# A GLA + RWKV-7 layer on one core: the state's share of y moved to array quarters at the end of a head pair

## The chip, the core and the metric

The kernel runs on one core of one Trainium2 chip, in one launch. The time is the device time of an execution in microseconds (us). The kernel before took 1492.62 us (median of 3 runs, 1492.28 to 1493.64).

A core has five engines with a queue each. The profile calls them PE (TensorE, matrix products; PEld is its loading of weights), DVE (VectorE), ACT (ScalarE), POOL (GpSimd) and SP (SyncE, which here issues the DMAs). A queue is worked off in order. Matrix products land in PSUM, eight banks of 128 partitions by 512 float32; the other operands lie in SBUF.

## What is computed

One layer of a decoder over 1024 prompt tokens and 8 single-token samples, width 1024, all in float32:

- `p = x @ w_in`, 9360 columns, split into the inputs of two branches and two gates.
- a gated linear attention branch (GLA) with 4 heads;
- an RWKV-7 branch with 16 heads of 64: for every token `S = S (diag(w) - kk^T (kk * a)) + v^T k` and `y = S r`, where `w = exp(-0.606531 * sigmoid(...))` is a decay for each channel. Then y is normalised, scaled, and a bonus is added;
- both branches are multiplied by `silu` of their gates, projected up, merged under sigmoid gates, projected by `w_out`, and normalised with the residual.

Outputs are y for prompt and samples, and the final states of both branches.

## The kernel before

**Tiling.** Tokens run along the free dimension, channels on the 128 partitions. There are two passes: 512 prompt tokens and the 8 samples, then 512 prompt tokens. Large products split each float32 operand into two parts of TensorE's faster 32-bit format (`xh`, `xl` of x; a two-part `wpart` of the weights) and add three products. They are the `proj<-xh,wpart` and `proj<-xl,wpart` groups of the profile.

**The RWKV branch.** Two heads make a pair, head 0 on partitions 0 to 63 and head 1 on 64 to 127. There are 8 pairs a pass, 16 in all. A pair's 512 tokens are cut into 8 chunks of 64 (`NCH`, `C`). Within a chunk the recurrence is solved as a block system, so that only the state goes from chunk to chunk. A pair goes through these functions:

- `front` (L1128 on). Sigmoids give the decay's logarithm; a scan along each chunk sums it (`tb`, started anew at each chunk by the mask `reset`); `Pc`, with 65 columns a chunk, is `exp` of minus the sum from the chunk's start, and `tb` becomes `exp` of plus the sum. `AZ` holds, for each chunk, three slots of 64 columns: the removal key times its decay, r of head 0 and r of head 1 times theirs. The last two are each zero on the other head's partitions; those zeros are written once at the start. `BK` holds the two right-hand factors divided by their decay, `pc` the decay over a whole chunk. Then the masked matrices: for 4 chunks at a time, two banks (one for each head) take 8 matmuls on 64 rows of the array, and VectorE multiplies them by a mask into `GG` (tile `gg`). Corner blocks of `GG` go through memory (`LD`) to POOL, which solves them token by token; the result returns to `XT`.
- `back` completes the inverse, and copies slot 0 of `AZ` over the diagonal blocks of `GG[:, :, 0]` (the off-diagonal ones hold the masked matrix).
- `turn` transposes `BK` and v. `d.u` is a tile of [128, chunk, head, 65]: on a head's partitions, under its own index, lies the state, and on the other partitions lies v.
- `chain` (L1303 on) goes through the chunks in order. For each: `pr = GG[:, x, 0] . u`, copied to `rh`; `pY = u . AZ[:, x, 1:]`, one full-array matmul of 128 rows, 128 columns and 128 streamed columns, which is the state's share of y for both heads (thanks to the zeros); `s0`, the state times `pc`, on ScalarE; `pu = XT . rh`, copied into u; `pS = BK . u`; and the next state, `pS * pc + s0`. `pY` keeps two PSUM banks for the length of a chain. When all chunks are done, 16 matmuls on column halves of the array (`pY<-gg,wide`) add the tokens' share of y in one uninterrupted group, and four copies bring y to SBUF.
- `norm` normalises y and stores it to `o_rwkv`, which is read again much later for the up-projection.

**Order.** Nothing in the program's text fixes the order between streams. `Order.run` is a planner: each stream (`pair`, `chain`, `evacuate`, GLA `head`, weight loads `w`, projections `block` and so on) offers its next operation, `price` estimates its duration, `start` the moment at which operands, buffers and engine are free, and the operation with the earliest start less its priority is written next into its engine's queue. The constants at the top (`HOP`, `PRIO`, `FOR_PE`, `SCARCE`, `URGENT` and others) are what it weighs. Operations of `E` may go to DVE or POOL, those of `C` to ACT or DVE. `together` makes one operation of a list of matmuls, so that nothing comes between them. `SWITCH` is the planner's price for a change of the array's tiling.

**Buffers.** `SBUF` names the tags and counts; `row` ([128, 520], 38 of them) serves nearly everything. `BANKS` shares out the PSUM banks: 2 `proj`, 3 `big`, 1 `pch` for the chain, 2 `pY`. `get(tag, n)` waits until n buffers are free at once; `get_of` takes the free one of several tags.

Of the kernel before, what the change touches and what calls it, by code (L numbers as in the profile page):

```python
# [20 lines left out]
P = 128  # L21
D = 1024
# [25 lines left out]
    "row": ([P, HALF], 38), "wide": ([P, NCH * 2 * CV], 4), "gg": ([P, 4 * HT], 2), "lw": ([P, HT], 2),  # L48
    "l2s": ([P, 2 * P], 1), "pc": ([P, NCH], 3), "X": ([P, 256], 1),
    "Xt": ([P, P], 1), "Ld": ([P, P], 2), "S": ([P, GDV], 2), "Sp": ([P, CV], 2), "s0p": ([P, 2 * CV], 2), "rh": ([P, 2 * CV], 2), "vm": ([P, NCH], 2),  # L50
# [5 lines left out]
BANKS = {"proj": 2, "big": 3, "pch": 1, "pY": 2}  # L56

KEEP = 3
# [7 lines left out]
SPARE_ROWS = 10  # L66
EARLY_GATES = 11


HOP = {"P": 0.2, "D": 0.339, "G": 0.12, "V": 0.064, "A": 0.14}  # L70
# [5 lines left out]
AGE = 0.851  # L76

SPARE = 0.315
LANDED = 0.337
BIAS = 0.174  # L80
ASIDE = 1.32

PRIO = {"evacuate": 0.48, "pair": 0.3, "turn": 0.5, "chain": 0.5, "norm": 0.1, "x": 0.69, "lora": 0.08, "rank":
        -0.15, "head": 0.3, "gate": -0.13, "w": 0.3, "out": -0.17, "state": 0.16, "block": 0.09}
FOR_PE = {"pair": 0.92, "turn": 1.49, "chain": 1.0, "norm": 0.76, "lora": 0.29, "rank": 1.96, "head": 1.0, "gate":
        1.0, "state": 1.85, "out": 0.05}
STAND, SCARCE, PER_ROW = 0.034, 0.227, 0.083

URGENT = 0.981
# [61 lines left out]
def price(eng, name, out, args, ins):  # L151

    n = out.free_size()
    src = [x for x in ins if x.tensor.space != PSUM] if eng == "A" else ins
    if eng == "P":
        m = args[0].free_size()
        rows, cols = tiles(name, args)
        if name == "transpose":
            return 0.1095
        if args[0].dtype == F32R:  # L160
            return max(m / 1200, 0.0045 + n / 2256) if rows == cols == P else (m + n) / 1200
        if rows == cols == P:
# [266 lines left out]
class Kern(Order):  # L429
# [71 lines left out]
    def setup(self):  # L501
# [64 lines left out]
        self.reset = cp.tile([P, HT], U8, name="reset")  # L566
        nc.vector.memset(self.reset, 1)
        nc.vector.memset(self.reset[:, ::C], 0)


        for tag, n, bufs in (("az", 3 * HT, 2), ("XT", 2 * HT, 2), ("Yd", HT, 1), ("Xd", HT, 1)):
# [132 lines left out]
    def blocks(self):  # L704
        xs = None
        for b in self.plan:
# [17 lines left out]
            for tt, (t0, n) in enumerate(tiles):  # L724
                fin = tt == len(tiles) - 1
                ps = yield from (self.get("proj") if b.src is self.a["w_in"] else self.get_of("proj", "pY", "big"))
# [19 lines left out]
    def first_blocks(self, xs):  # L746

        run = []
        for b in self.plan[:2]:
            evac = yield from b.act()  # L750
            for tt, (t0, n) in enumerate(b.c.tiles):
                ps = yield from self.get_of("proj", "pY", "big")
# [375 lines left out]
    def front(self, c, p, st, d):  # L1128
# [4 lines left out]
        AZ, GG = az.rearrange("p (c s t) -> p c s t", c=NCH, s=3), gg.rearrange("p (c k h t) -> p c k h t", c=NCH, k=2, h=2)  # L1133
# [14 lines left out]
        ta, tb, td, te = (x[:, :HT] for x in (ta, tb, td, te))  # L1148
        Pc_ = Pc_[:, :NCH * (C + 1)]
        Pc = Pc_.rearrange("p (c t) -> p c t", t=C + 1)  # L1150
# [3 lines left out]
        yield A.activation(ta, pw, AF.Sigmoid, bias=self.pvec("w0", p))  # L1154
# [19 lines left out]
        for h, hs in enumerate(HS):  # L1174
            yield E.tensor_mul(AZ[hs, :, 1 + h], bc(r)[hs], Pc[hs, :, 1:])
        pc = yield from self.get("pc")
        yield E.tensor_copy(pc, Pc[:, :, C])

        for h, hs in enumerate(HS):
            yield E.tensor_mul(BK[hs, :, h * C:h * C + C], bc(td)[hs], bc(tb)[hs])  # L1180
            yield E.tensor_mul(BK[hs, :, C - h * C:2 * C - h * C], bc(kb)[hs], bc(tb)[hs])
# [67 lines left out]
    def back(self, d):  # L1249
# [24 lines left out]
        for h, hs in enumerate(HS):  # L1274
            yield self.C.copy(GG[hs, :, 0, h], d.AZ[hs, :, 0])
# [27 lines left out]
    def chain(self, c, p, d):  # L1303
# [9 lines left out]
        S, pYs = (yield from self.get("Sp")), []  # L1313

        for x in range(NCH):
            u = u_[:, x]
            uf = u.rearrange("p h v -> p (h v)")[:, 1:1 + P]
            if x % 4 == 0:
                pYs.append((yield from self.bank("pY", [P, 4, 2, C])))
# [21 lines left out]
            self.free(pS, s0p)  # L1341
        uf = u_.rearrange("p c h v -> p c (h v)")
        yield together([self.P.matmul(pYs[x // 4][hs, x % 4, h], uf[:, x, 1 + h * C:1 + h * C + C], GG[:, x, 1, h], start=False,
                                      stop=True, skip_group_check=True) for x in range(NCH) for h, hs in enumerate(HS)])
        for x, pY in enumerate(pYs):
            cs = slice(4 * C * x, 4 * C * x + 4 * C)
            for h, hs in enumerate(HS):
                yield self.C.copy(d.y[hs, cs].rearrange("p (c t) -> p c t", t=C), pY[hs, :, h])
            self.free(pY)
# [199 lines left out]
    def load_out(self):  # L1549
# [4 lines left out]
        ln1 = yield from self.get("Yd")  # L1554
        self.lnv = [[ln[:, 0:512], ln[:, 512:D]], [ln[:, D:], ln1]]
# [27 lines left out]
    def out(self, c, xs):  # L1583
# [3 lines left out]
        for t0, x0 in rows:  # L1587
# [6 lines left out]
            for n, (c0, cn) in enumerate(parts):  # L1594
                ps = yield from self.get_of("proj", "pY", "big")
# [22 lines left out]
    def out_sample(self, xs):  # L1618
# [10 lines left out]
        for j in range(2):  # L1629
            ps = yield from self.get_of("proj", "pY", "big")  # L1630
# [205 lines left out]
```

## Time and profile before

| | |
|---|---|
| median of 3 runs | 1492.62 us |
| profiled execution | 1492.24 us |
| its span, first to last instruction | 1490.5 us |
| busy PE / DVE / ACT / POOL | 1472.6 / 1068.1 / 820.8 / 399.7 us |
| granted TensorE clock, mean | 0.998 of full speed |
| DMA | 319.08 MB, mean 214 GB/s |

A row of groups of instructions reads: line, engine, operation, output<-inputs by tile names, tiling of the array where it is a matmul (rows*columns), shape, count | busy us, mean ns of one | idle time of the engine before them and who ended it. Nearly all instructions carry L225, the planner's helper, so tiles tell them apart. A float32 matmul leaves two records, one for each of its passes. Matmuls are pipelined: a record's own duration contains the depth of the pipeline, and the pace is read from starts. A row of stretches reads: from:to, length, then busy us and count for PE, PEld, DVE, ACT and POOL, granted clock, DMA share and GB/s.

### The profile page before, as it was taken

The page shows a single profiled execution, that of the slowest core. Times are in us where ns is not written, and L with a number is a line of the kernel's source. Part 1 is how long each engine was busy: PE and PEld are TensorE (multiplying, and loading weights), DVE is VectorE, ACT ScalarE, POOL GpSimd, SP SyncE. Part 2 cuts the span into 40 slices and gives each one's busy share as a digit, 9 for nine tenths or more (in the row PEclk, how much of TensorE's full clock was granted, in tenths as well). Part 3 has the DMA queues.
Part 4 walks back from the last instruction along what each step waited for, and adds up shares of the span by engine and source line. Part 5 has one row for each costly group of instructions (what it writes and reads, how often), then busy time and mean ns, then how long its engine had stood idle before and what let it go on. Part 6 is the DMA issues. An engine that isn't in the chain of part 4 may idle for free.

```text
span 1490.5 us, 29705 instructions
## 1 busy us (share of the span) xinstructions
PE 1472.6 (99%) x10308; PEld 1304.6 (88%) x10308; DVE 1068.1 (72%) x2196; ACT 820.8 (55%) x2098; POOL 399.7 (27%) x1154
## 2 busy tenths in 40 slices
PE   9999999999999999999999999999999999999997
PEld 8899999999999998788887888888888898897786
DVE  6688688858796788766557696978586846566665
ACT  5646766766676667544644464464456555643210
POOL 1060605133503442064223505140523050000000
PEclk9999999999999999999999999999999999999999
DMA  8786886787668875764555465746564868787432
GB/s 295 255 285 215 274 280 207 247 263 267 219 195 268 290 248 177 239 203 137 175 182 172 140 184 192 215 131 209 186 219 144 250 185 282 259 293 241 142 113 85
DMA packets 211312, 319.08 MB, mean 214 GB/s; under 512 B 91699, under 2 KB 107196, under 8 KB 211164
## 3 DMA queue, kind: packets, MB, share of 16 engines
q1 hardware_dynamic: 211164, 317.20, 66.3%
q8 instruction: 82, 1.34, 0.4%
q14 instruction: 66, 0.54, 0.1%
HBM read 197.45 MB, written 118.61 MB: 212 GB/s over the span
## 4 chain that ended last, share of the span: by engine, by line
PE 89%; DVE 4%; DMA 3%; SPq 1%; issue 1%; ACT 1%; POOL 0%; POOLq 0%; DVEq 0%; ACTq 0%
PE proj L225 56%; PE big L225 19%; PE pY L225 8%; PE pch L225 6%; DVE row L225 1%; SPq L225 1%; DVE wpart L225 1%; DVE wide L225 1%; DMA row<-w_out 0%; DMA wraw<-w_in 0%; DMA row<-lora 0%; DMA row<-xT 0%; ACT wpart L225 0%; DMA wide<-Sp 0%; DMA row<-mg 0%
## 5 line engine op out<-in xcount | busy, mean ns | idle before, releaser
L225 PE MATMUL proj<-xh,wpart 128*128 128x264 f32 (+2 forms) x3744 | 914.0, 328 | 1.6 <-DVE row L225 1.1
L225 PEld LDWEIGHTS proj<-xh,wpart 128*128 128x128 f32 x3744 | 623.9, 189 | 51.9 <-issue 4.0
L225 PE MATMUL proj<-xl,wpart 128*128 128x264 f32 (+2 forms) x1872 | 616.1, 329 | 0.0
L225 PEld LDWEIGHTS proj<-xl,wpart 128*128 128x128 f32 x1872 | 353.6, 189 | 25.0 <-issue 2.4
L225 POOL TENSOR_TENSOR Xt<-X,wide 128x60 f32<-128x60 f32 (+24 forms) x496 | 168.0, 339 | 483.4 <-DMA wide<-LD 172.8
L225 DVE TENSOR_TENSOR wpart<-wraw,wpart 128x512 fp32r<-128x512 f32 x209 | 147.0, 705 | 67.8 <-ACT wpart L225 63.1
L225 ACT CAST wpart<-wraw 128x512 fp32r<-128x512 f32 x210 | 130.2, 621 | 113.5 <-PE proj L225 68.3
L225 DVE TENSOR_TENSOR row<-row 128x512 f32<-128x512 f32 (+10 forms) x343 | 178.6, 532 | 13.2 <-ACT row L225 6.9
L225 POOL TENSOR_TENSOR X<-X,Xt 128x60 f32<-128x60 f32 (+24 forms) x496 | 173.5, 350 | 38.6
L225 ACT ACTIVATE row<-row 128x512 f32<-128x512 f32 (+4 forms) x229 | 137.9, 611 | 19.8 <-DMA row<-sg 8.4
L225 DVE SCALAR_TENSOR_TENSOR wide<-pch,pc,s0p 64x65 f32<-64x65 f32 x224 | 63.3, 283 | 82.7 <-PE pch L225 80.1
L225 ACT COPY rh<-pch 128x130 f32<-128x130 f32 x125 | 33.5, 268 | 126.1 <-PE pch L225 125.6
L225 DVE SCALAR_TENSOR_TENSOR row<-proj,pv,row 128x255 f32<-128x255 f32 (+1 forms) x97 | 55.5, 572 | 48.5 <-ACT tail L225 33.3
L225 POOL TENSOR_TENSOR row<-row 128x256 f32<-128x256 f32 (+3 forms) x26 | 28.1, 1090 | 227.7 <-DVE row L225 125.6
L225 PE MATMUL big<-row 128*128 128x128 f32 (+4 forms) x464 | 84.8, 316 | 0.5 <-DMA row<-lora 0.5
L225 ACT COPY wide<-pch 64x65 f32<-64x65 f32 x244 | 50.6, 207 | 57.7 <-PE pch L225 53.0
L225 ACT ACTIVATE row<-proj,omu 128x256 f32<-128x256 f32 (+1 forms) x97 | 53.0, 547 | 49.6 <-PE proj L225 47.0
L225 POOL TENSOR_SCALAR XT<-XT,st 128x256 f32<-128x256 f32 x1 | 1.2, 1223 | 267.2 <-ACT st L225 267.2
L225 PE MATMUL big<-xh,wpart 128*128 128x512 f32 (+2 forms) x288 | 68.9, 323 | 0.0
L225 PEld LDWEIGHTS big<-row 128*128 128x128 f32 (+3 forms) x464 | 59.6, 175 | 7.6 <-ACT row L225 1.7
L407 ACT ACT_TABLE_LOAD x50 | 64.2, 1283 | 0.9
L225 PE MATMUL pY<-xh,wpart 128*128 128x256 f32 (+2 forms) x240 | 56.9, 317 | 1.3 <-ACT wpart L225 1.1
(269 smaller groups left out, 2360.7 us busy)
## 6 DMA issues: line engine op xcount, KB each, us to landing
w<-wpart SPq DMA_DIRECT2D x146, 512.0 KB
wpart<-w SPq DMA_DIRECT2D x146, 512.0 KB
wraw<-w_in SPq DMA_DIRECT2D x146, 256.0 KB
wide<-LD SPq DMA_DIRECT2D x64, 128.0 KB
wraw<-w_up_gla SPq DMA_DIRECT2D x32, 256.0 KB
wraw<-w_up_rwkv SPq DMA_DIRECT2D x32, 256.0 KB
sg<-row SPq DMA_DIRECT2D x16, 260.0 KB
row<-sg SPq DMA_DIRECT2D x16, 260.0 KB
```

Source lines behind the costliest of these rows:

```text
L225: ways.append((eng, lambda call=call: call(out, *args, **kw), price(eng, name, out, args, ins)))
L407: self.nc.scalar.preload_act_table_set(self.table)
```

## The change

The decay factors of a pair are now taken relative to a chunk's **end**. The scan runs backwards over 65 columns a chunk (the 65th is set to zero), `Pc` is `exp` of plus the sum, `tb` of minus it, and `pc` is the first column of `tb`. `AZ` has two slots, its zeros are no longer needed, and r is multiplied for both heads in one instruction.

In `chain` the full-array `pY` matmul is gone. `s0` (state times `pc`) is kept for every chunk: it is written over `GG[:, x, 0]`, which the chunk's first matmul has read by then (`gg` gets 65 columns for 64 to hold it). At the end of the chain 16 matmuls of 64 rows, 64 columns and 64 streamed columns, one for each chunk and head, give the state's share of y. They stand in one group with the 16 half-column matmuls of before, into one `big` bank taken only then, and one copy brings y out. `AZ`'s removal keys are multiplied by `pc` when they are put into `GG`, and the next state is a plain sum.

The masked matrices of a pair are made in one group of 16 matmuls over four banks at once, where there were two groups of 8 over two banks each. Beside that: `big` has 5 banks and `pY` none, `row` has 40 buffers, `KEEP` is 0, `SPARE_ROWS` and `EARLY_GATES` are one more, the tag `s0p` is gone, the planner's constants are others, and `price` has a case for 64 by 64. The tiles for the last normalisation's weights follow `az`'s new size (`Yd` and `Xd` in place of the third part of `az`).

```diff
-    "row": ([P, HALF], 38), "wide": ([P, NCH * 2 * CV], 4), "gg": ([P, 4 * HT], 2), "lw": ([P, HT], 2),
+    "row": ([P, HALF], 40), "wide": ([P, NCH * 2 * CV], 4), "gg": ([P, NCH * 4 * CV], 2), "lw": ([P, HT], 2),
...
-BANKS = {"proj": 2, "big": 3, "pch": 1, "pY": 2}
-KEEP = 3
+BANKS = {"proj": 2, "big": 5, "pch": 1}
+KEEP = 0
...
-        return 0.1365 if cols == P else (0.0625 if cols == 64 else 0.142 if n > P else 0.088) if rows == P else 0.5
+        return 0.1365 if cols == P else (0.0625 if cols == 64 else 0.142 if n > P else 0.088) if rows == P else 0.0625 if rows == cols == 64 else 0.5
...
-        yield V.tensor_tensor_scan(tb, self.reset, ta, 0.0, ALU.mult, ALU.add)
-        yield E.memset(Pc[:, :, 0:1], 1.0)
+        yield V.tensor_tensor_scan(tb[:, ::-1], self.reset, ts[:, ::-1], 0.0, ALU.mult, ALU.add)
...
-        yield A.activation(Pc[:, :, 1:], bc(tb), AF.Exp, scale=-LAM)
-        yield A.activation(tb, tb, AF.Exp, scale=LAM)
+        yield A.activation(Pc_, tb, AF.Exp, scale=LAM)
+        yield A.activation(tb, tb, AF.Exp, scale=-LAM)
...
+        yield E.tensor_mul(AZ[:, :, 1], bc(r), Pc[:, :, 1:])
...
-        for h, hs in enumerate(HS):
-            yield E.tensor_mul(AZ[hs, :, 1 + h], bc(r)[hs], Pc[hs, :, 1:])
...
-        for x in range(0, NCH, H):
-            ps = yield from self.get("big", 2)
-            ps = [y.rearrange("p (c k t) -> p c k t", c=H, k=2) for y in ps]
-            yield together([self.P.matmul(ps[h][:, n], BK[hs, x + n], AZ[hs, x + n, 0:2 + h:1 + h], start=True, stop=True)
-                            for n in range(H) for h, hs in enumerate(HS)])
-            for h in range(2):
-                yield V.tensor_mul(GG[:, x:x + H, :, h], ps[h], mk[:, :, h].unsqueeze(1).to_broadcast([P, H, 2, C]))
-            self.free(*ps)
+        ps = yield from self.get("big", 4)
+        p4 = [y.rearrange("p (c k t) -> p c k t", c=H, k=2) for y in ps]
+        yield together([self.P.matmul(p4[2 * (n // H) + h][:, n % H], BK[hs, n], AZ[hs, n], start=True, stop=True)
+                        for n in range(NCH) for h, hs in enumerate(HS)])
+        for n, y in enumerate(p4):
+            x, h = H * (n // 2), n % 2
+            yield V.tensor_mul(GG[:, x:x + H, :, h], y, mk[:, :, h].unsqueeze(1).to_broadcast([P, H, 2, C]))
+            self.free(ps[n])
...
-            yield self.C.copy(GG[hs, :, 0, h], d.AZ[hs, :, 0])
+            yield self.E.tensor_mul(GG[hs, :, 0, h], d.AZ[hs, :, 0], d.pc[hs].unsqueeze(2).to_broadcast([C, NCH, C]))
...
-            yield self.P.matmul(pYs[-1][:, x % 4], uf, AZ[:, x, 1:], start=(x % 4 == 0), stop=False,
-                                skip_group_check=True)
-            s0p = yield from self.get("s0p")
-            s0 = s0p.rearrange("p (h v) -> p h v", h=2)
             yield A.activation(s0, u, AF.Copy, scale=pc[:, x:x + 1])
...
-                yield V.scalar_tensor_tensor(un, pS[hs, h], pc[hs, x:x + 1], s0[hs, h], ALU.mult, ALU.add)
+                yield V.tensor_add(un, pS[hs, h], s0[hs, h])
...
+        pY = yield from self.bank("big", [P, NCH, C])
+        vs = [slice(1 + h * C, 1 + h * C + C) for h in range(2)]
+        yield together([self.P.matmul(pY[hs, x], d.s0[hs, x, vs[h]], AZ[hs, x, 1], start=(x == 0), stop=False, skip_group_check=True)
+                        for x in range(NCH) for h, hs in enumerate(HS)] +
+                       [self.P.matmul(pY[hs, x], uf[:, x, vs[h]], GG[:, x, 1, h], start=False, stop=True, skip_group_check=True)
+                        for x in range(NCH) for h, hs in enumerate(HS)])
+        yield self.C.copy(d.y, pY.rearrange("p c t -> p (c t)"))
```

More of the change, by code (lines that the diff above doesn't have):

```diff
@@ L47 @@
 SBUF = {
-    "row": ([P, HALF], 38), "wide": ([P, NCH * 2 * CV], 4), "gg": ([P, 4 * HT], 2), "lw": ([P, HT], 2),
-    "l2s": ([P, 2 * P], 1), "pc": ([P, NCH], 3), "X": ([P, 256], 1),
-    "Xt": ([P, P], 1), "Ld": ([P, P], 2), "S": ([P, GDV], 2), "Sp": ([P, CV], 2), "s0p": ([P, 2 * CV], 2), "rh": ([P, 2 * CV], 2), "vm": ([P, NCH], 2),
+    "row": ([P, HALF], 40), "wide": ([P, NCH * 2 * CV], 4), "gg": ([P, NCH * 4 * CV], 2), "lw": ([P, HT], 2),
+    "l2s": ([P, 2 * P], 1), "pc": ([P, NCH], 3), "az": ([P, 2 * HT], 2), "X": ([P, 256], 1),
+    "Xt": ([P, P], 1), "Ld": ([P, P], 2), "S": ([P, GDV], 2), "Sp": ([P, CV], 2), "rh": ([P, 2 * CV], 2), "vm": ([P, NCH], 2),
     "sto": ([P, P], 1), "bnd": ([P, 1], 3), "st": ([P, 32], 3), "part": ([P, HALF], 2), "l2p": ([P, 2 * P], 2),
@@ L65 @@
 RANKW, RANKM = 48, 66
-SPARE_ROWS = 10
-EARLY_GATES = 11
-HOP = {"P": 0.2, "D": 0.339, "G": 0.12, "V": 0.064, "A": 0.14}
+SPARE_ROWS = 11
+EARLY_GATES = 12
+HOP = {"P": 0.2, "D": 0.418, "G": 0.115, "V": 0.064, "A": 0.14}
 SWITCH = 0.092
@@ L74 @@
 TABLE = 1.28
[L76 to L89, printed above, removed]
+AGE = 1.045
+SPARE = 0.411
+LANDED = 0.456
+BIAS = 0.193
+ASIDE = 3.641
+PRIO = {"evacuate": 0.39, "pair": 0.3, "turn": 0.5, "chain": 0.42, "norm": 0.1, "x": 0.61, "lora": 0.42, "rank":
+        0.32, "head": 0.27, "gate": -0.38, "w": 0.3, "out": -0.01, "state": -0.13, "block": -0.38}
+FOR_PE = {"pair": 1.0, "turn": 1.63, "chain": 0.8, "norm": 0.39, "lora": 0.29, "rank": 1.85, "head": 0.89, "gate":
+        1.0, "state": 2.12, "out": 0.05}
+STAND, SCARCE, PER_ROW = 0.034, 0.249, 0.23
+URGENT = 2.315
 SIGMOID, EXP = "sigmoid_and_others", "natural_log_exp_and_others"
@@ L565, in setup @@
         self.shT = cp.tile([P, NRC, NS], F32, name="shT")
-        self.reset = cp.tile([P, HT], U8, name="reset")
+        self.reset = cp.tile([P, NCH * (C + 1)], U8, name="reset")
         nc.vector.memset(self.reset, 1)
-        nc.vector.memset(self.reset[:, ::C], 0)
-        for tag, n, bufs in (("az", 3 * HT, 2), ("XT", 2 * HT, 2), ("Yd", HT, 1), ("Xd", HT, 1)):
+        nc.vector.memset(self.reset[:, ::C + 1], 0)
+        for tag, n, bufs in (("XT", 2 * HT, 2), ("Yd", HT, 1), ("Xd", HT, 1)):
             ts = [cp.tile([P, n], F32, name=f"{tag}{i}") for i in range(bufs)]
@@ L725, in blocks @@
                 fin = tt == len(tiles) - 1
-                ps = yield from (self.get("proj") if b.src is self.a["w_in"] else self.get_of("proj", "pY", "big"))
+                ps = yield from (self.get("proj") if b.src is self.a["w_in"] else self.get_of("proj", "big"))
                 q = ps[:, :n]
@@ L751, in first_blocks @@
             for tt, (t0, n) in enumerate(b.c.tiles):
-                ps = yield from self.get_of("proj", "pY", "big")
+                ps = yield from self.get_of("proj", "big")
                 run.append((b, tt, t0, n, ps, evac))
@@ L1132, in front @@
         BK = BK_[:, :2 * HT].rearrange("p (c t) -> p c t", c=NCH)
-        AZ, GG = az.rearrange("p (c s t) -> p c s t", c=NCH, s=3), gg.rearrange("p (c k h t) -> p c k h t", c=NCH, k=2, h=2)
+        AZ, g4 = az.rearrange("p (c s t) -> p c s t", c=NCH, s=2), gg.rearrange("p (c k z) -> p c k z", c=NCH, k=2)
+        GG, d.s0 = g4[:, :, :, :P].rearrange("p c k (h t) -> p c k h t", h=2), g4[:, :, 0]
         yield lambda: self.l2s
@@ L1147, in front @@
         ta, tb, td, te, Pc_ = yield from self.rows(5)
-        ta, tb, td, te = (x[:, :HT] for x in (ta, tb, td, te))
-        Pc_ = Pc_[:, :NCH * (C + 1)]
-        Pc = Pc_.rearrange("p (c t) -> p c t", t=C + 1)
+        ts, tb, Pc_ = (x[:, :NCH * (C + 1)] for x in (ta, tb, Pc_))
+        ta, td, te = (x[:, :HT] for x in (ta, td, te))
+        ts3, tb3, Pc = (x.rearrange("p (c t) -> p c t", t=C + 1) for x in (ts, tb, Pc_))
         yield A.activation(te, kb, AF.Square, scale=self.pvec("kk", p))
@@ L1153, in front @@
         yield from lora(pw, 0)
-        yield A.activation(ta, pw, AF.Sigmoid, bias=self.pvec("w0", p))
+        yield E.memset(ts3[:, :, C:], 0.0)
+        yield A.activation(ts3[:, :, :C], bc(pw), AF.Sigmoid, bias=self.pvec("w0", p))
         self.free(pw)
@@ L1173, in front @@
         yield E.tensor_mul(kb, kb, te)
+        yield E.tensor_mul(AZ[:, :, 1], bc(r), Pc[:, :, 1:])
+        pc = yield from self.get("pc")
+        yield E.tensor_copy(pc, tb3[:, :, 0])
         for h, hs in enumerate(HS):
-            yield E.tensor_mul(AZ[hs, :, 1 + h], bc(r)[hs], Pc[hs, :, 1:])
-        pc = yield from self.get("pc")
-        yield E.tensor_copy(pc, Pc[:, :, C])
-        for h, hs in enumerate(HS):
-            yield E.tensor_mul(BK[hs, :, h * C:h * C + C], bc(td)[hs], bc(tb)[hs])
-            yield E.tensor_mul(BK[hs, :, C - h * C:2 * C - h * C], bc(kb)[hs], bc(tb)[hs])
+            yield E.tensor_mul(BK[hs, :, h * C:h * C + C], bc(td)[hs], tb3[hs, :, 1:])
+            yield E.tensor_mul(BK[hs, :, C - h * C:2 * C - h * C], bc(kb)[hs], tb3[hs, :, 1:])
         yield V.scalar_tensor_tensor(te, r, self.pvec("rk", p), kb, ALU.mult, ALU.mult)
@@ L1312, in chain @@
                 yield self.E.memset(u_[hs, 0, h], 0.0)
-        S, pYs = (yield from self.get("Sp")), []
+        S = yield from self.get("Sp")
+        uf = u_.rearrange("p c h v -> p c (h v)")
         for x in range(NCH):
[L1316 to L1319, printed above, removed]
+            u, s0 = u_[:, x], d.s0[:, x].rearrange("p (h v) -> p h v", h=2)
             pr = yield from self.bank("pch", [P, 2, CV])
@@ L1339, in chain @@
                 un = u_[hs, x + 1, h] if x + 1 < NCH else S[hs]
-                yield V.scalar_tensor_tensor(un, pS[hs, h], pc[hs, x:x + 1], s0[hs, h], ALU.mult, ALU.add)
[L1341 to L1349, printed above, removed]
+                yield V.tensor_add(un, pS[hs, h], s0[hs, h])
+            self.free(pS)
+        pY = yield from self.bank("big", [P, NCH, C])
[5 more added lines that the diff above has]
+        yield self.C.copy(d.y, pY.rearrange("p c t -> p (c t)"))
+        self.free(pY)
         self.free(AZ, BK, u_, GG, XT, pc)
@@ L1553, in load_out @@
         yield lambda: self.backs == 2 * NPAIR
-        ln1 = yield from self.get("Yd")
-        self.lnv = [[ln[:, 0:512], ln[:, 512:D]], [ln[:, D:], ln1]]
+        y, x = (yield from self.get("Yd")), (yield from self.get("Xd"))
+        self.lnv = [[ln[:, 0:512], ln[:, 512:D]], [y, x]]
         for j in range(2):
@@ L1594, in out @@
             for n, (c0, cn) in enumerate(parts):
-                ps = yield from self.get_of("proj", "pY", "big")
+                ps = yield from self.get_of("proj", "big")
                 q = ps[:, :cn]
@@ L1629, in out_sample @@
         for j in range(2):
-            ps = yield from self.get_of("proj", "pY", "big")
+            ps = yield from self.get_of("proj", "big")
             for k in range(NK):
```

## The prediction

> **What bounds the kernel now.** I read the page's busy shares first, then the chain that ended last, then stretches of the span, then who makes TensorE wait, and last the single instructions that the change touches.
>
> ```profile
> span 1490.5 us, 29705 instructions
> PE 1472.6 (99%) x10308; PEld 1304.6 (88%) x10308; DVE 1068.1 (72%) x2196; ACT 820.8 (55%) x2098; POOL 399.7 (27%) x1154
> ...
> PE 89%; DVE 4%; DMA 3%; SPq 1%; issue 1%; ACT 1%; POOL 0%; POOLq 0%; DVEq 0%; ACTq 0%
> ```
>
> ```profile
> 0.00:50.00 50.00, 46.01 (x327) 42.84 (x328) 31.22 (x75) 29.07 (x64) 6.83 (x17) 0.97 0.82 287
> ...
> 1450.00:1490.50 40.50, 32.84 (x165) 27.43 (x163) 21.55 (x36) 1.99 (x8) 2.77 (x3) 0.95 0.24 83
> sum 1490.50, PE 1472.61 PEld 1304.62 DVE 1068.08 ACT 820.79 POOL 399.66; mean PE 122.72 PEld 108.72 DVE 89.01 ACT 68.40 POOL 33.31
> ```
>
> TensorE (PE) is idle for 1490.50 - 1472.61 = 17.9 us. Of these 50.00 - 46.01 = 4.0 lie in the first 50 us and 40.50 - 32.84 = 7.7 in the last 40 (the final normalisation and its store), so 6.2 us are left for the 1400 us between. The largest single causes are small:
>
> ```profile
> PE pch L225 <- DVE wide L225: 1.2, 3, 0.6
> PE proj L225 <- DVE row L225: 1.1, 1, 1.1
> PE pY L225 <- ACT wpart L225: 1.1, 1, 1.1
> ```
>
> (total us, times, longest.) So the end is set by the amount of work in TensorE's queue. A busy PE need not be a PE at its peak, so each price below is taken from starts of neighbouring instructions, not from busy time. What takes a microsecond out of that queue shortens the run by about a microsecond; what moves on DVE, ACT or POOL costs nothing while these are at 72, 55 and 27%.
>
> **The change part by part.** *State's share of y.* Now each of a pair's eight chunks has a full-array matmul `pY<-az,wide`, 128 rows by 128 columns, 128 columns streamed. It goes, and two matmuls on 64 by 64 quarters with 64 columns come in its place, all sixteen of a pair together just ahead of the sixteen existing `pY<-gg,wide`. The counts (a float32 matmul leaves two records, one for each pass):
>
> ```profile
> L225 PE MATMUL pY<-az,wide 128*128 128x128 f32 x256 | 49.3, 274 | 0.0
> L225 PE MATMUL big<-az,wide 64*128 64x128 f32 x512 | 37.6, 285 | 0.8 <-DVE row L225 0.6 <-DVE gg L225 0.2
> L225 PE MATMUL pY<-gg,wide 128*64 128x64 f32 x512 | 18.4, 225 | 0.0
> ```
>
> Hence 128 full-array matmuls in 16 pairs, 8 a pair. Their price, from TensorE in order of time (start us, us, instruction, records):
>
> ```profile
> 604.23 0.39 PE L225 MATMUL pch<-wide,gg 128*128 128x130 f32 x2
> 604.45 0.39 PE L225 MATMUL pY<-az,wide 128*128 128x128 f32 x2
> 604.59 0.48 PE L225 MATMUL proj<-xh,wpart 128*128 128x512 f32 x1
> 604.91 0.39 PE L225 MATMUL proj<-xl,wpart 128*128 128x512 f32 x1
> 605.14 0.39 PE L225 MATMUL proj<-xh,wpart 128*128 128x512 f32 x1
> ```
>
> A projection pass takes 605.14 - 604.91 = 0.23 us. The pY matmul and the projection pass behind it take 604.91 - 604.45 = 0.46 together (the projection's start at 604.59 is drawn early, and the next instruction shows the true pace), so pY costs 0.46 - 0.23 = 0.23 us, two passes of 0.115. Removed a pair: 8 x 0.23 = 1.84 us.
>
> *What small tiles cost.* The trace has half-row tiles (the masked matrices, `big<-az,wide`) and half-column tiles (`pY<-gg,wide`), each in a group of its own:
>
> ```profile
> 608.15 0.39 PE L225 MATMUL pch<-wide,gg 128*128 128x130 f32 x2
> ...
> 610.98 0.39 PE L225 MATMUL pch<-wide 128*128 128x130 f32 x2
> 611.29 1.16 PE L225 MATMUL big<-az,wide 64*128 64x128 f32 x16
> 612.38 0.49 PE L225 MATMUL pch<-wide,gg 128*128 128x130 f32 x2
> 612.71 0.39 PE L225 MATMUL pY<-az,wide 128*128 128x128 f32 x2
> ```
>
> ```profile
> 1290.44 0.62 PE L225 MATMUL proj<-xh,wpart 128*128 128x512 f32 x2
> 1290.99 1.15 PE L225 MATMUL pY<-gg,wide 128*64 128x64 f32 x32
> 1292.07 0.50 PE L225 MATMUL proj<-xl,wpart 128*128 128x512 f32 x1
> 1292.41 0.62 PE L225 MATMUL proj<-xh,wpart 128*128 128x512 f32 x2
> ```
>
> The masked group takes the queue from 610.98 + 0.23 = 611.21 to 612.71 - 0.23 = 612.48, that is 1.27 us. Its 16 records are 8 side-by-side couples (two row halves at once) of 128 columns, 8 x 0.115 = 0.92; the other 0.35 us is the price of changing the array's tiling and changing it back. The `pY<-gg` group goes from 1290.44 + 2 x 0.23 = 1290.90 to 1292.41 - 0.23 = 1292.18, 1.28 us; less the same 0.35, its 16 couples of 64 columns cost 0.93, or 0.058 each, half of 0.115 for half the columns. Both readings fit only if the two halves run at once.
>
> *Quarters.* No 64 by 64 tile is in the trace. Sixteen quarter matmuls are 32 records; if the quarter of head 0 (rows and columns 0 to 63) runs beside that of head 1 (64 to 127), they are 16 couples of 64 columns and cost 0.93 us, the price of the `pY<-gg` group. If they run one after the other they cost twice that, 1.86. I take 0.93: halves of rows and halves of columns both pair up in the trace, and a diagonal quarter differs from its neighbour in both. The tiling also changes once more, from quarters to half columns inside the group: at least nothing, at most a whole 0.35, and I take one change of the two, 0.35 / 2 = 0.175.
>
> One rule speaks against 0.93. The Trainium skill, "TensorEngine Tiling (Array Packing)", section Restrictions and Gotchas, says that different row tiles cannot access the same PSUM bank at one time. Here both quarters write into one bank; by that rule they could not overlap, and the term would be 1.86. "PSUM — Partial Sum Buffer" in the same skill, section PSUM bank collisions raise a hardware error, narrows what was measured to the same bank and the same group of 32 partitions, which the two heads do not share; by that the term is 0.93. In this trace the masked group's row halves go to two banks and the `pY<-gg` column halves to one bank from full rows, so neither page is tested here.
>
> *Masked matrices in one group.* Two groups of 16 records a pair become one of 32 over four banks. The work stays; one change of tiling and back goes: 0.35 us a pair. The lower bound is zero, if another small-tile group had stood beside it; in the rows above full-array matmuls stand on both sides.
>
> *The sum on TensorE.* A pair: -1.84 + 0.93 + 0.175 - 0.35 = -1.085 us; 16 pairs: -17.4 us. The profiled execution took 1492.24 us (1490.5 span and 1.7 around it), 0.4 under the median of the runs, 1492.62. 1492.24 - 17.4 = **1474.8 us**. With the unknown change of tiling at its ends (0 and 0.35) it is 1472.0 and 1477.6.
>
> *The other engines.* Their prices before:
>
> ```profile
> L225 DVE SCALAR_TENSOR_TENSOR wide<-pch,pc,s0p 64x65 f32<-64x65 f32 x224 | 63.3, 283 | 82.7 <-PE pch L225 80.1
> L225 ACT COPY rh<-pch 128x130 f32<-128x130 f32 x125 | 33.5, 268 | 126.1 <-PE pch L225 125.6
> L225 ACT COPY row<-pY 64x256 f32<-64x256 f32 x64 | 23.5, 367 | 10.1 <-PE pY L225 9.4
> L225 DVE TENSOR_TENSOR az<-row 64x512 f32<-64x512 f32 x32 | 22.1, 689 | 0.3
> L225 DVE COPY gg<-az 64x512 f32<-64x512 f32 x30 | 12.5, 418 | 0.3
> L225 DVE TENSOR_TENSOR az<-row 128x512 f32<-128x512 f32 x16 | 11.2, 697 | 0.1
> ```
>
> r times its factor is one full-height product in place of two half-height ones (0.70 for 1.38 us). The copy of the first matrix's diagonal blocks becomes a product (2 x 0.69 for 2 x 0.42, +0.54). Four copies of y (4 x 0.37 = 1.47) become one of 128 x 512, which I bound by 0.37 below and 0.70 above. A chunk's state update loses its scalar (0.28 at most, and not dearer). The scan and two exponentials grow from 512 to 520 columns. Taken together that is a gain of about a microsecond a pair on engines that do not set the end, so nothing. The scaled state s0 is now written over the chunk's own block of `gg`, and so has to wait for the matmul that read it; the copy of `rh` on ACT (0.27 us) waits for that same matmul and stands ahead of s0 in the queue, so nothing is later. The y copies are the only step that comes later, by the quarters' 1.1 us at the end of a chain.
>
> ```profile
> L225 PE MATMUL pY<-az,wide x256: 270/274/318, 139.9 to 1287.6; 128*128 128x128 f32 x128
> ```
>
> A chunk takes 612.38 - 608.15 = 4.2 us, a chain eight of these, 34 us, and the sixteen chains lie between 139.9 and 1287.6 us, one every 72: this is covered, and the cover's size is in the third rival below. No DMA is added or moved between queues, and SP and POOL get no new waits; two zero fills of `az` leave POOL at the start.
>
> *Buffers and order.* Two rows more, five common banks for three and two, no reserve of rows for row-takers, and new constants of the planner: the order of every engine is written anew. I put this at zero. Its gain cannot exceed the 6.2 us of idle time in the middle; its loss is bounded by nothing in the trace, and I take the same 6 us as its likely size.
>
> **The rivals.** *Quarters one after the other.* For it: in the trace row halves that run at once write to two banks, and the quarters share one. Against it: both kinds of half tile pair up. Price 16 x 0.93 = 14.9 us more: 1489.7 us, 2.5 us under the profiled time, which is no measurable change.
>
> *Waits in the middle go too.* More rows and one pool of banks let projections run further ahead. 1474.8 - 6.2 = 1468.6 at most. For it: the waits are on rows and on weight parts. Against: they are 1 us each and of many kinds, and a new order makes new ones.
>
> *Slower: the pairs fall behind.* The masked group takes four of five banks at once, which the GLA heads, the two lora products and the head sums also draw on; a pair's front then waits until four are free together. If the delay adds up along the pairs, the last pair stores its output late:
>
> ```profile
> L225 SPq DMA_DIRECT2D row<-o_rwkv x8: 423/430/432, 1323.8 to 1339.7; - x8
> L225 SPq DMA_DIRECT2D o_rwkv<-row x1: 319/319/319, 1305.8 to 1305.8; - x1
> ```
>
> The last store is issued at 1305.8 and first read back at 1323.8, so the first 18 us cost nothing. From there TensorE runs dry microsecond for microsecond, and the run is slower than before once the lag passes 18 + 17.4 = 35.4 us, 2.2 us a pair; at 2.5 us a pair (40 us) the time is 1492.24 - 17.4 + 22 = 1497. Against it: two of the five banks were held through a chain's 34 us before and are no longer, and a group's four banks are needed for some 4 us (1.5 us on TensorE and four masks at about 0.7 on DVE).
>
> **How the numbers follow.** Less than 0.2% (3.0 us) is what a measurement of this kernel cannot tell from no change. Forecast, TensorE's sum with small waits either way: 0.75, 1469 to 1481 (6 us either way, the middle's idle time). Waits go as well, below that: 0.08. Quarters in series: 0.10, at the edge of no change. Pairs fall behind: 0.07, of which 0.05 ends slower and 0.02 about even. Faster 0.75 + 0.08 + 0.03 of the series case = 0.86; the same 0.07 + 0.02 = 0.09; slower 0.05. The range leaves out the series case, the slower one and the far end of the waits, and is 2 us wider than the likeliest case's own for the change of tiling that I could only halve: 1467 to 1483.
>
> **What would show it.** In the profile after: `pY<-az,wide` with full tiles gone; 512 records of 64*64 form, in couples, a pair's two end groups lasting about 2.4 us from the first start to the next full-array matmul (3.3 if the quarters run in series); one masked group of 32 records a pair taking about 2.2 us where two took 2.5; PE busy near 1455 us and its idle time still near 18. I would be wrong if the quarters' starts stand 0.058 us apart one by one, if PE's idle time grows by more than 6 us, or if the last o_rwkv store comes after its reader wants it.

## The result, and the profile after

The changed kernel takes 1469.62 us (median of 4 runs, 1468.74 to 1471.1), the kernel before in the same comparison 1493.13. The ratio is 0.9846 with a 95% interval of 0.9833 to 0.9859: 23.5 us, 1.5%, faster. The prediction was 1474.8 with a range of 1467 to 1483. The profiled execution of the changed kernel took 1470.01 us. Its page:

```profile
span 1468.0 us, 30054 instructions
PE 1451.1 (99%) x10564; PEld 1292.3 (88%) x10564; DVE 1053.4 (72%) x2202; ACT 816.6 (56%) x2067; POOL 362.5 (25%) x1117
...
PE 89%; DVE 2%; DMA 2%; SPq 1%; ACT 1%; issue 0%; POOL 0%; POOLq 0%; DVEq 0%; ACTq 0%
```

The span is shorter by 22.5 us and PE's busy time by 21.5; the rest is idle time, 17.9 before and 16.9 now. The stretches (length, then PE's busy time first) show where the idle time lies:

```profile
0.00:50.00 50.00, 44.17 (x309) 41.03 (x310) 29.20 (x71) 27.68 (x61) 4.20 (x15) 0.93 0.82 281
...
1427.50:1468.00 40.50, 32.88 (x166) 27.49 (x164) 21.64 (x37) 1.99 (x8) 2.77 (x3) 0.97 0.23 84
sum 1468.00, PE 1451.06 PEld 1292.33 DVE 1053.36 ACT 816.55 POOL 362.47; mean PE 120.92 PEld 107.69 DVE 87.78 ACT 68.05 POOL 30.21
```

The start now idles 5.8 us (4.0 before) and the end 7.6 (7.7), so the middle went from 6.2 to 3.5 us. Now come the groups that were changed, first by their counts:

```profile
L225 PE MATMUL big<-az,wide 64*128 64x128 f32 x512 | 32.9, 278 | 0.0
L225 PE MATMUL big<-gg,wide 128*64 128x64 f32 x512 | 18.4, 225 | 0.0
L225 PE MATMUL big<-az,gg 64*64 64x64 f32 x512 | 18.4, 221 | 0.0
```

The full-array `pY<-az,wide` is gone. The quarters (`big<-az,gg`) have 512 records and the same busy time as the half columns. The end of a chain, and a masked group, on TensorE in order of time (start us, us, instruction, records):

```profile
615.26 0.38 PE L225 MATMUL pch<-wide 128*128 128x130 f32 x2
615.58 1.15 PE L225 MATMUL big<-az,gg 64*64 64x64 f32 x32
616.66 1.15 PE L225 MATMUL big<-gg,wide 128*64 128x64 f32 x32
617.74 0.73 PE L225 MATMUL proj<-xh,wpart 128*128 128x512 f32 x2
```

```profile
204.88 0.28 PE L225 MATMUL proj<-xl,wpart 128*128 128x256 f32 x1
205.09 2.06 PE L225 MATMUL big<-az,wide 64*128 64x128 f32 x32
207.08 0.49 PE L225 MATMUL pch<-wide,gg 128*128 128x130 f32 x2
207.32 0.48 PE L225 MATMUL proj<-xh,wpart 128*128 128x256 f32 x2
207.64 0.28 PE L225 MATMUL proj<-xl,wpart 128*128 128x256 f32 x1
```

The 32 quarter records take 616.66 - 615.58 = 1.08 us to the next group, exactly what the 32 half-column records behind them take (617.74 - 616.66); every pair whose records stand together in the trace shows 1.08 for the quarters. At 16 couples of 0.058 (the prediction's figure) that is 0.93 and 0.15 for the change of tiling; a run below measures that change apart. The masked group takes 207.08 - 205.09 = 1.99 us where two groups took 1.09 each. Ahead of it 205.09 - 204.88 = 0.21 us go by for one 256-column pass (0.12), so the way in costs 0.09. Behind it 207.64 - 207.08 = 0.56 go by for a chain matmul and two such passes (0.23 + 2 x 0.115), so the restart costs 0.10. Each group pays both.

### The profile page after: what moved, and what is told of

Its sections match the earlier page's. It is cut to its first block, busy times and chain, and to the rows that moved or that the text cites. A ratio compares the mean times of both kernels' runs of the same rounds, so it can differ in the third digit from the quotient of the medians.

```text
span 1468.0 us, 30054 instructions
## 1 busy us (share of the span) xinstructions
PE 1451.1 (99%) x10564; PEld 1292.3 (88%) x10564; DVE 1053.4 (72%) x2202; ACT 816.6 (56%) x2067; POOL 362.5 (25%) x1117
## 4 chain that ended last, share of the span: by engine, by line
PE 89%; DVE 2%; DMA 2%; SPq 1%; ACT 1%; issue 0%; POOL 0%; POOLq 0%; DVEq 0%; ACTq 0%
PE proj L225 56%; PE big L225 27%; PE pch L225 6%; SPq L225 1%; DVE row L225 1%; DMA wraw<-w_in 1%; DMA row<-o_gla 0%; DMA gla_s<-row 0%; DVE wpart L225 0%; DMA row<-o_rwkv 0%; ACT wpart L225 0%; ACT row L225 0%; POOL XT L225 0%; DVE xl L225 0%; DVE st L225 0%
## 5 line engine op out<-in xcount | busy, mean ns | idle before, releaser
L225 DVE TENSOR_TENSOR row<-row 128x512 f32<-128x512 f32 (+9 forms) x369 | 190.0, 527 | 9.1 <-ACT row L225 4.2
L225 ACT ACTIVATE row<-row 128x520 f32<-128x520 f32 (+4 forms) x229 | 137.7, 611 | 8.3 <-DMA row<-sg 3.1
L225 PE MATMUL big<-xh,wpart 128*128 128x512 f32 (+2 forms) x528 | 128.9, 329 | 0.5 <-ACT xh L225 0.5
L225 DVE TENSOR_TENSOR wide<-pch,gg 64x65 f32<-64x65 f32 x224 | 49.7, 222 | 77.5 <-PE pch L225 75.1
L225 ACT COPY row<-big 128x128 f32<-128x128 f32 (+7 forms) x151 | 50.4, 357 | 90.2 <-PE big L225 88.4
L225 PEld LDWEIGHTS big<-xh,wpart 128*128 128x128 f32 x528 | 89.8, 191 | 7.8 <-ACT xh L225 0.7
L225 PE MATMUL big<-xl,wpart 128*128 128x264 f32 (+2 forms) x264 | 87.0, 330 | 1.5 <-DVE xl L225 1.5
L225 PE MATMUL big<-row 128*128 128x128 f32 (+3 forms) x456 | 82.1, 316 | 0.3 <-DVE row L225 0.3
```

The costliest lines, as they stand in the source:

```text
L225: ways.append((eng, lambda call=call: call(out, *args, **kw), price(eng, name, out, args, ins)))
```

## The experiments

The theory: the gain is work taken out of TensorE's queue (about 18 us) and some waits. The rivals: the quarters add nothing of their own; buffers and the order of the work made the difference. All runs compute the whole layer. Each time is a median of at least 4 runs; the kernel before took 1492.4 to 1493.2 us beside them. The changed kernel itself ran only in the first comparison, so a distance from its 1469.62 is one between comparisons; taken from the ratios instead, these distances differ by up to 1.7 us.

### Quarters issued head by head

```diff
-                        for x in range(NCH) for h, hs in enumerate(HS)] +
+                        for h, hs in enumerate(HS) for x in range(NCH)] +
```

> The changed kernel with the 16 quarter matmuls of a pair issued head by head (8 of head 0, then 8 of head 1) instead of alternating; the same matmuls, the same order of everything else. Theory (the two diagonal quarters run side by side, 0.058 us a couple): neighbours now share a quarter and run one after the other, 32 records at about 0.058, +0.93 us a pair, +14.9 us: 1484.5. Rival (they were in series all along, or pair up whatever the order): 1469.6 within 1.

Measured 1482.65 us, ratio to the kernel before 0.9927 [0.9909, 0.9945]: 13.0 us slower than the changed kernel. TensorE at the end of a chain:

```profile
618.26 0.38 PE L225 MATMUL pch<-wide 128*128 128x130 f32 x2
618.58 1.90 PE L225 MATMUL big<-az,gg 64*64 64x64 f32 x32
620.40 1.15 PE L225 MATMUL big<-gg,wide 128*64 128x64 f32 x32
621.49 0.73 PE L225 MATMUL proj<-xh,wpart 128*128 128x512 f32 x2
```

The quarters now take 620.40 - 618.58 = 1.82 us instead of 1.08: 0.74 a pair, 11.8 us in all; PE's busy time grew by 12.1 (to 1463.2) and the span by 12.0 (to 1480.0). So the two diagonal quarters do run side by side when they alternate, and that is worth 12 to 13 us here. The expected 14.9 was too much because passes that follow one another on one quarter take (1.82 - 0.15) / 32 = 0.052 us each, less than a couple's 0.058.

### Two more changes of tiling

```diff
-        yield together([ ... 16 quarters ... ] + [ ... 16 half columns ... ])
+        yield together(qs[:8] + gs[:8] + qs[8:] + gs[8:])
```

> The changed kernel with a pair's end group in the sequence 8 quarters, 8 half columns, 8 quarters, 8 half columns (16 and 16 in the changed kernel); the same matmuls and the same order of everything else. It prices a change of the array's tiling by itself: two more a pair. From the changed kernel's trace 32 quarter records and the change behind them take 1.08 us, of which 0.93 are 16 couples at 0.058, so 0.15 a change: +2 x 16 x 0.15 = 4.8 us, 1474.4. Rival (a change inside a group is free, and only the way to and from full tiles costs): 1469.6 within 1.

Measured 1474.9 us, 0.987 [0.9851, 0.989], 5.3 us slower than the changed kernel; 4.8 was expected. In the trace:

```profile
615.42 0.68 PE L225 MATMUL big<-az,gg 64*64 64x64 f32 x16
616.03 0.69 PE L225 MATMUL big<-gg,wide 128*64 128x64 f32 x16
616.64 0.68 PE L225 MATMUL big<-az,gg 64*64 64x64 f32 x16
617.26 0.69 PE L225 MATMUL big<-gg,wide 128*64 128x64 f32 x16
617.87 0.73 PE L225 MATMUL proj<-xh,wpart 128*128 128x512 f32 x2
```

Half a group takes 0.61 to 0.62 us, twice that 1.23 against 1.08: 0.15 us a change. This does not lean on the 0.058: eight couples more take 1.08 - 0.61 = 0.47, which is 0.059 a couple. PE's busy time rose from 1451.1 to 1456.9 and the span from 1468.0 to 1473.2. With the same order everywhere else, a microsecond on TensorE is a microsecond of the run.

### The masked matrices in two groups again

```diff
-        ps = yield from self.get("big", 4)
...
+        for x in range(0, NCH, H):
+            ps = yield from self.get("big", 2)
...
```

> The changed kernel with one part undone: the masked matrices again in two groups of 8 matmuls over two banks each. Theory (the gain is TensorE's work and its changes of tiling): one more change of tiling and back a pair. A group of 16 records lasted 1.09 us to the next instruction before, the merged one of 32 records 1.98; with the way in (0.09) and the slow first pass behind it (0.10) two groups cost 0.39 us more a pair, 16 x 0.39 = 6.3 us: 1475.9 against 1469.6. Rival (the gain is in buffers and the order, and the grouping is hidden): 1469.6 within 2.

Measured 1500.31 us, 1.005 [1.0034, 1.0066]: 31 us slower than the changed kernel, slower even than the kernel before. Neither expectation holds. Here the planner wrote a new order, and its waits (total us, times, longest) begin with one that has nothing to do with the masks:

```profile
PE big L225 <- ACT xh L225: 13.7, 3, 9.5
```

That is the up-projection of the RWKV branch waiting for its input. The program reads `o_rwkv` back only when the pairs of the pass and the samples' recurrence are both through (L1739). The stores of the samples' states and of the branch's output, and the reads of that output, of this run,

```profile
L225 SPq DMA_DIRECT2D rwkv_s<-row x8: 338/428/588, 879.8 to 1262.5; - x8
...
L225 SPq DMA_DIRECT2D o_rwkv<-row x17: 319/367/966, 232.9 to 1287.1; - x17
L225 SPq DMA_DIRECT2D row<-o_rwkv x16: 319/430/652, 1291.7 to 1348.7; - x16
```

and of the changed kernel,

```profile
L225 SPq DMA_DIRECT2D rwkv_s<-row x8: 337/412/592, 856.3 to 1143.0; - x8
...
L225 SPq DMA_DIRECT2D row<-o_rwkv x16: 422/430/1232, 1248.3 to 1316.2; - x16
```

show the samples' last state 120 us later (1262.5 against 1143.0) and the first read 43 us later (1291.7 against 1248.3); TensorE then stood idle for 9.5 us up to 1295.1. In all its idle time grew by 18.5 us (to 35.4) and its busy time by 13.6 (to 1464.7). The edit's own price had to be found another way (below).

### The planner's constants exchanged, and nudged

```diff
-HOP, AGE, SPARE, LANDED, BIAS, ASIDE, PRIO, FOR_PE, SCARCE, PER_ROW, URGENT, KEEP, SPARE_ROWS, EARLY_GATES of the one kernel
+... those of the other
```

> The changed kernel with every constant of the planner, KEEP, SPARE_ROWS and EARLY_GATES as in the kernel before; rows, banks and the work stay as changed. Theory (some 18 us of the gain are TensorE's work, the 4 to 5 above that are fewer waits from the new order): 1472 to 1476, PE's busy time within 3 us of 1451. Rival (the order matters much more than the work): over 1480. Rival (the constants do nothing): 1469.6 within 1.

> The kernel before, its work, rows and banks as they were, with the planner's constants, KEEP, SPARE_ROWS and EARLY_GATES of the changed kernel; the mirror of the run with the old constants on the new work. Theory (a set of constants fits one kernel's work, and any other set lets waits grow): 1498 to 1515, PE idle over 25 us. Rival (the new constants are simply better): under 1490.

The new work with the old constants: 1538.49 us, 1.031 [1.0291, 1.033]. The old work with the new constants: 1502.8 us, 1.0053 [1.0036, 1.0069]. The second is what its theory expected, with 1501.2 - 1474.1 = 27.1 us of idle time. The first is the rival's "over 1480" by far. Its page, its waits, and TensorE in the stretch where it loses most:

```profile
span 1535.6 us, 30098 instructions
PE 1476.6 (96%) x10564; PEld 1303.1 (85%) x10564; DVE 1047.4 (68%) x2193; ACT 807.8 (53%) x2042; POOL 403.3 (26%) x1149
```

```profile
PE proj L225 <- ACT xh L225: 9.7, 1, 9.7
```

```profile
1356.87 0.77 PE L225 MATMUL pch<-wide,gg 128*128 128x130 f32 x2 [0.64 <-DVE wide L225]
1357.99 0.80 PE L225 MATMUL pch<-rh,XT 128*128 128x130 f32 x2 [0.36 <-ACT rh L225]
1359.37 0.80 PE L225 MATMUL pch<-wide 128*128 128x130 f32 x2 [0.57 <-ACT wide L225]
...
1376.91 0.80 PE L225 MATMUL proj<-xh,wpart 128*128 128x512 f32 x1 [9.69 <-ACT xh L225]
```

The last pair's chain stands alone on TensorE with nothing to fill its waits, and behind it the projection waits 9.7 us for that pair's output, which is stored and read back at once:

```profile
1371.45 0.33 SPq L225 DMA_DIRECT2D o_rwkv<-row  x1
...
1372.30 1.88 SPq L225 DMA_DIRECT2D row<-o_rwkv  x4
```

This is the prediction's third rival, pairs that fall behind; but the same four-bank group is in the changed kernel, where the last `o_rwkv` store is issued at 1283.1 and that pass is first read at 1301.3. The order written by the old constants made the difference; four banks at once do not do it by themselves.

The granted clock fell as well. In the same stretch (third number from the end of a row) it was 0.68, 0.67 and 0.50:

```profile
1350.00:1360.00 10.00, 5.53 (x19) 3.49 (x17) 3.46 (x9) 5.97 (x17) 0.00 (x0) 0.68 0.84 287
1360.00:1370.00 10.00, 5.20 (x68) 4.06 (x67) 2.98 (x8) 6.78 (x11) 0.00 (x0) 0.67 0.22 74
1370.00:1380.00 10.00, 3.09 (x7) 2.17 (x8) 5.37 (x8) 3.55 (x6) 0.00 (x0) 0.50 0.74 255
```

Here 32 quarter records take 1.90 us to the next group (1360.10 to 1362.00) in place of 1.08. So the loss is more than idle time: idle time grew by 42 us over the changed kernel's, and busy time by 25.5 (1476.6 against 1451.1) for the same work. An estimate, busy time times what the clock lacked of 1 in each stretch of 10 us of both runs, puts some 15 of these 25.5 down to the clock. The same estimate gives some 6 of the 13.6 in the earlier run with two masked groups.

Then two constants moved by under 2%:

```diff
-AGE = 1.045
+AGE = 1.04
...
-BIAS = 0.193
+BIAS = 0.19
```

> The changed kernel with two of the planner's constants moved by under 2% (BIAS 0.193 to 0.19, AGE 1.045 to 1.04); work, rows and banks the same. It measures how far the time moves when the order is only written anew. Theory (the order reacts to anything; the shipped one is a picked one): 1472 to 1480. Rival (the order is steady, and the 31 and 69 us of the runs before have other causes): 1469.6 within 1.5.

Measured 1477.44 us, 0.9891 [0.9875, 0.9906]: 7.8 us slower for no change of the work. So a comparison of two edits whose order is written anew can carry some 8 us of accident (this is one nudge, no more were run), and far more where the constants were made for other work. (The runs with quarters head by head and with the tilings twice kept the order, so they carry none of this.)

### The same search for four kernels

To compare work with work, priorities and weights (`PRIO`, `FOR_PE`, `AGE`, `BIAS`, `ASIDE`, `STAND`, `SCARCE`, `PER_ROW`, `URGENT`) were drawn anew for four kernels (some 1,700 sets for the changed one), and the set with the earliest end by the planner's own arithmetic taken; the latencies that it assumes (`HOP`, `SPARE`, `LANDED`) were the changed kernel's in all four. Each kernel keeps its own rows, banks and `KEEP`. Three of the four follow here, the last in the next section; all ran in one comparison, in which the kernel before took 1492.74 us.

> The changed kernel (work, rows, banks) with priorities and weights of the planner picked anew: some 1,700 sets drawn around the shipped one, and the set with the earliest end by the planner's own arithmetic taken. This run and the three with it have the same search behind them, so their differences are less a matter of a lucky order. Theory: the shipped order of the changed kernel is near its best, 1467 to 1473. Rival (much is still to be had from the order): under 1462.

> The kernel before (work, rows, banks) with priorities and weights found by the same search. Theory (18 us between the two kernels are TensorE's work, whatever the order; 4 to 5 were order): 1484 to 1490, 16 to 20 us above the changed kernel with the same search. Rival (the gain was mostly a better order): within 8 us of it.

> The changed kernel with the masked matrices in two groups of 8 matmuls (the first experiment) and priorities and weights found by the same search. Theory (the 31 us of the first experiment were 6.3 of tiling changes and 25 of an order that no longer fitted): 5 to 9 us above the changed kernel with the same search. Rival (four banks at once and one group matter in themselves): 20 us or more above it.

| kernel | us | ratio to the kernel before |
|---|---|---|
| changed, searched | 1469.25 | 0.9841 [0.9826, 0.9855] |
| before, searched | 1486.48 | 0.9958 [0.9941, 0.9975] |
| changed with two masked groups, searched | 1482.18 | 0.9925 [0.9908, 0.9942] |

The shipped order of the changed kernel was as good as the searched one (1469.62 and 1469.25), that of the kernel before was not: it had 6.3 us to give (1492.74 - 1486.48). Between the two kernels with the same search lie 17.2 us, as expected; this is the price of work, rows and banks together, with one search each, so that some accident of order is left in it. The third row stands 12.9 us above the first, which is neither the 5 to 9 of its theory nor the 20 of its rival. Pages of the changed kernel, of the kernel before and of the one with two groups, all searched:

```profile
span 1468.6 us, 30061 instructions
PE 1451.3 (99%) x10564; PEld 1292.8 (88%) x10564; DVE 1052.8 (72%) x2198; ACT 815.0 (55%) x2067; POOL 370.2 (25%) x1121
```

```profile
span 1484.1 us, 29688 instructions
PE 1471.1 (99%) x10308; PEld 1302.0 (88%) x10308; DVE 1058.2 (71%) x2166; ACT 845.3 (57%) x2155; POOL 369.8 (25%) x1133
```

```profile
span 1477.2 us, 30068 instructions
PE 1457.3 (99%) x10564; PEld 1291.8 (87%) x10564; DVE 1054.5 (71%) x2216; ACT 799.2 (54%) x2044; POOL 359.4 (24%) x1122
```

Between the kernel before and the changed one PE's busy time differs by 19.8 us (1471.1 and 1451.3), while idle time is 4.3 higher in the changed one (17.3 and 13.0). The search thus took 17.9 - 13.0 = 4.9 us of idle time and 1.5 us of busy time out of the kernel before.

With two masked groups busy time is 6.0 us higher, near the 6.3 expected of the tiling changes; idle time adds 2.6 (19.9 against 17.3). This profiled execution, at 1478.99 us, was the fastest of that kernel's runs, and that of the changed kernel, at 1470.38, the slowest of its own; the 4 us between 8.6 in the spans and 12.9 in the medians are not explained. So 6 of the 12.9 are tiling changes, and whether the rest is accident of order or a price of the grouping itself stays open. The 31 us of the first attempt were mostly order.

### Four quarters at once

```diff
-        pY = yield from self.bank("big", [P, NCH, C])
+        pYs = (yield from self.bank("big", [P, NCH // 2, C])), (yield from self.bank("big", [P, NCH // 2, C]))
...
+        at = [(n, e, h if not e else 1 - h) for n in range(NCH // 2) for e in range(2) for h in range(2)]
+        yield together([self.P.matmul(pYs[e][HS[h ^ e], n], d.s0[HS[h], 2 * n + e, vs[h]], AZ[HS[h], 2 * n + e, 1],
+                                      start=(n == 0), stop=False, skip_group_check=True) for n, e, h in at] +
...
+        y4 = d.y.rearrange("p (n e t) -> p n e t", e=2, t=C)
+        yield self.C.copy(y4[:, :, 0], pYs[0])
+        for h, hs in enumerate(HS):
+            yield self.C.copy(y4[hs, :, 1], pYs[1][HS[1 - h]])
```

> The changed kernel with the shares of y of odd chunks put on the other head's half of the partitions, in a second bank, so that four neighbouring quarter matmuls sit on four different quarters; y comes out with three copies for one. Theory (quarters on different rows and columns run at once and only their own streams limit them): four at once, 0.47 us for the 16 in place of 0.93, -7.4 us: 1462. Rival (two streams at once is what the array takes, or weights loading limits): 1469.6 within 2.

Measured 1469.3 us, 0.9846 [0.9828, 0.9865], no faster: the rival's time, but not for the rival's reason. PE's busy time fell from 1451.1 to 1446.1, and idle time rose from 16.9 to 25.1 (span 1471.2; this profiled execution was the slowest of its four, 4 us above the median). With the search:

> The four-quarter version (odd chunks' shares of y on the other half of the partitions) with priorities and weights found by the same search, and a quarter matmul priced at 0.0315 us in the planner. Theory (its group is 0.45 us shorter a pair, 16 x 0.45 = 7.3 us, and the earlier run lost that to waits of an unfitted order): 5 to 9 us below the changed kernel with the same search, so 1461 to 1465. Rival (its two banks and three copies cost as much as it saves): no faster than the changed kernel with the same search.

Measured **1463.92 us**, 0.9805 [0.9791, 0.982], 5.3 us below the changed kernel with the same search, and faster than both kernels of this case. Its page and the end of one of its chains (L220 is the helper's line here, since the constants take fewer lines):

```profile
span 1461.9 us, 30110 instructions
PE 1443.7 (99%) x10564; PEld 1283.4 (88%) x10564; DVE 1055.3 (72%) x2193; ACT 811.3 (55%) x2094; POOL 375.9 (26%) x1121
```

```profile
636.08 0.38 PE L220 MATMUL pch<-wide 128*128 128x130 f32 x2
636.39 0.70 PE L220 MATMUL big<-az,gg 64*64 64x64 f32 x32
637.02 1.15 PE L220 MATMUL big<-gg,wide 128*64 128x64 f32 x32
638.10 0.50 PE L220 MATMUL proj<-xl,wpart 128*128 128x512 f32 x1
```

The quarters take 637.02 - 636.39 = 0.63 us for the same 32 records, 0.45 less than 1.08: 7.2 us over 16 pairs, and busy time is lower by 7.6 than in the searched changed kernel. All four quarters work at once. Of the 7.6, idle time took back 0.9 by the spans (18.2 against 17.3). The medians show 5.3; what accident of order and the spread of the runs have in the difference is not separated.

## Why the prediction was right, and where it was not

- **TensorE's queue sets the end.** Right. Where the order was kept, busy time and span rose together: by 12.1 and 12.0 us with the quarters in series, by 5.8 and 5.2 with two more changes of tiling.
- **The full-array matmul, 1.84 us a pair, and 0.93 for the quarters.** The quarters measured 0.93 (1.08 less the change of tiling, which the run that doubled it puts at 0.15). No run measured the full-array matmul by itself.
- **The extra change of tiling, 0.175.** It is 0.15, from the run that doubled it.
- **The masked matrices in one group, -0.35.** The new group shows 1.99 for twice 1.09, that is 0.19, and one way in and one slow restart (0.09 and 0.10) are saved besides: 0.38. The searched pair gives 6.0 us of busy time, 0.375 a pair.
- **The sum.** With these sizes it is -1.84 + 0.93 + 0.15 - 0.38 = -1.14 a pair, -18.2 us. The two kernels with the same search differ by 17.2.
- **Buffers and order: "I put this at zero".** This term was wrong. The gain came out 6.1 us above the 17.4 of the sum, and by the pair with the same search 6.3 of the 23.5 us are order: the kernel before had that much left in its order, the changed kernel nearly nothing. The range held the time because it had been made wide for waits, not because the sum knew of this. The bound on the gain, 6.2 us of idle time in the middle, came out about right in size, but what the search gained did not all come from there: 1.5 us were busy time. On the side of loss, 6 us as a likely size was too small: the same work loses 69 us with the old constants and 8 with two constants nudged. That the constants had been changed with the work was what made the sum of TensorE's terms come true; as far as the prediction goes, which only set 6 us of gain against 6 of loss, that was luck.
- **Busy time.** The prediction expected near 1455 us; it was 1451.1, a fall of 21.5 where the terms add up to 18.2. With the same search the fall is 19.8. What the rest is stays open: waits too short to show as idle time, or a term a little too small.
- **Waits in the middle go too.** The measured 1469.62 lies near this rival's 1468.6. Its mechanism had a part only: the middle lost 2.7 of its 6.2 us of idle time, the first 50 us gained 1.8, and all idle time together fell by 1.0.
- **The signs.** A pair's end groups last 617.74 - 615.58 = 2.16 us where 2.4 were expected, and the masked group 1.99 where 2.2 were: the ways in and the slow restarts lie outside these starts. The last `o_rwkv` store still stands 18 us ahead of its reader (1283.1 and 1301.3).
- **The quarters in series.** Refuted; had it been so, the price would have been 12 to 13 us, not 14.9.
- **The pairs fall behind.** The mechanism is real, with the point from which it decides as stated (the last `o_rwkv` store against its reader), but four banks at once do not set it off by themselves; an unfitted order does.
- **The Trainium skill's rule on row tiles** ("TensorEngine Tiling (Array Packing)", Restrictions and Gotchas: different row tiles cannot access one PSUM bank at one time). The trace disagrees where they write to different partitions: both quarters write to one bank, and 32 records take 1.08 us, as many half columns of full rows take 1.08, and 1.82 when neighbours share a quarter. The narrower statement of "PSUM — Partial Sum Buffer" in the Trainium skill (PSUM bank collisions raise a hardware error), which that section gives as measured, for the same bank and same group of 32 partitions, fits; no run here put two row tiles on the same partitions of one bank.

## What to carry to other kernels

Where one queue sets the end, price an edit from the starts of neighbouring instructions in that queue, changes of tiling included, and compare it with runs that leave the order alone. Where a planner writes the order, an edit and its constants are one thing: measure both kernels with the same search behind them, or the accident of order (8 us for a nudge here, 31 and 69 for work its constants did not fit) hides or invents the gain. Idle time alone does not measure an order either: here a better order took 1.5 us out of busy time beside 4.9 of idle time, and an unfitted one added 25.5 us of busy time for the same work, by the estimate above some 15 of them because the granted clock had fallen.

## What the runs showed of the hardware that was not expected

All four 64 by 64 quarters run at once: 32 records in 0.63 us up to the next group, against 1.08 on two quarters and 1.82 when neighbours share a quarter. Each half of the partitions is written by two of the four, in two banks. Passes that follow one another on one quarter take 0.052 us each, a couple on two quarters 0.058, and four on four quarters (0.63 - 0.15) / 8 = 0.060 for the four, with the same 0.15 for the change of tiling. Two row halves of the array write to one bank at once, on different partitions, at the pace of half columns from full rows (1.08 us for 32 records, both). Where TensorE waited much, the granted clock in the profile fell to 0.50 to 0.68, and the same 32 records took 1.90 us.
